# Block norms of attention keys and queries: from one f32 product per segment to two fp32r products of a split square

## The chip, the cores and the metric

The kernel runs on one core of one Trainium2 chip. The metric is device microseconds of one execution, from runs of the whole kernel. The engines are named as the profile names them: PE (TensorE matmul), PEld (its weight load), DVE (VectorE), ACT (ScalarE), POOL (GpSimd) and SP (SyncE, which issues most DMAs).

## The reference

One layer of a hybrid backbone on 1280 tokens (256 context tokens, then 1024 latent tokens on a grid 64 wide) of width 1024. Modulated RMSNorm, one input projection, two head groups side by side, one output projection with a gated residual, then a SwiGLU feed-forward with its own gated residual.

```
q, k, v, z, a, b = ...                         # group A: gated DeltaNet, 4 heads of 128, both directions
o = delta(q, k, v) fwd + bwd                   # chunks, each with a triangular solve
q = rms_norm(q, q_norm_w) * NA_HEAD_DIM ** -0.5     # group B: neighbourhood attention, 8 heads of 64
k = rms_norm(k, k_norm_w)                      # mean of squares over the 64 channels of a head
out = softmax(q k^T + bias) v                  # window keys plus all context keys
```

The change is in the two `rms_norm` lines of group B. `rms_norm` divides by the root of the mean of squares over a head's 64 channels, per token.

## The kernel before, in words

Activations lie with channels on the 128 partitions and tokens along the free dimension. A matmul of two f32 operands is written either directly in f32, or as products of operands rounded to fp32r: the normalized input is held as a high and a low part (`hh`, `hl`, eight tiles each of 128 channels), and a weight as `whi`, `wlo` (`load_w`: ACT rounds at L199, POOL or DVE subtracts at L200). A projection block of 128 output channels then takes, for each of the eight input tiles, three products (`mm_part`, L405) into PSUM banks of the tag `blk`, one bank for each segment of tokens. Segments are 256, 512 and 512 tokens; queries have no context tokens and only the two of 512.

The projection is a list of jobs: DeltaNet key blocks k0 to k3 and a wide half of z, then attention keys nk0, nk1, nk2, half of nv (a wide job of values), nk3, DeltaNet queries q0 to q3, attention queries nq0 to nq3, and values. In the loop over jobs, job n's matmuls are emitted, with pieces of the finish of job n-2 (transposes, stores) and of a background list between them; then its banks are evacuated (L438, or L453 into a tile `cr` for a block that has a short convolution, which follows on DVE at L457 and L461), the norm of job n-1 is emitted, and job n's SiLU and square (`silu`, the square lands in a tile `r` of the tag `cr`).

The norm of an nk or nq block: for each segment, one f32 matmul with a block-diagonal mask of ones (two blocks of 64) sums the squares of each head (L492), ACT takes Ln of the bank (L493), then Exp with scale -0.5 (L497), DVE multiplies (L500), ACT and DVE make an f16 high and low part (L505, L506 for keys; L512, L513 for queries), and SP stores both. The banks for the sums have the tag `m`, two buffers, which the transposes and the DeltaNet work also use.

The background list, from nk0 on: `block_inverses`, which builds per-chunk triangular systems and solves them on DVE in a loop of 30 dependent pairs (L885, L887), transposes the result back on PE (L897), and copies it on ACT (L899), with two more multiplies and transposes on DVE (L905, L908); then `preps`, one for each chunk of 128 tokens: POOL masks four tiles `rg` (L957, after six memsets at L931), ACT fills `fx` (L961), PE forms the log decays (L967, L968), ACT takes Exp (L971), DVE multiplies (L974), PE and ACT apply one block of the inverse (L986, L989), and three rounds of small products follow (L997), each copied to `y` by DVE and ACT (L999, L1000) before the next round. The banks of `preps` have the tag `pr`, two buffers. Preps 0 and 1 may start as soon as the inverses are there; the others are held until all q blocks are done. A second background list computes modulation (L219, L221, L232, L234).

Nothing of this is an order written by hand to the end: a list scheduler orders the instructions of each engine, and a tile takes a free buffer of its tag, so a change of durations or of buffers changes the order of all of them. In the tag `cr` two buffers serve the evacuated block and the square; in the tag `kx` three buffers serve the f16 pair `hl16`, the transposed tiles and others.

Of the kernel before, what the change touches and what calls it, by code (L numbers as in the profile page):

```python
# [30 lines left out]
PLAIN = 2  # L31
SEGS = [(0, 256), (256, 512), (768, 512)]

C_ID, C_LE, C_GE, C_BD2, C_ONE = range(5)


def const_arrays():
    p = np.arange(128)[:, None]
    f = np.arange(128)[None, :]
    same = (p // 32) == (f // 32)  # L40
    m = [p == f, p <= f, p >= f, p > f, p < f, (p > f) & same, (p < f) & same]
    big = np.stack([x.astype(np.float32) for x in m[:3] + [(p // 64) == (f // 64)]], 1)
    f32 = np.arange(32)[None, :]
    q = p % 32
    small = np.stack([x.astype(np.float32) for x in
                      [q <= f32, q >= f32, q < f32, q > f32]], 1)
    out = np.concatenate([big.reshape(128, -1), small.reshape(128, -1)], 1)
    masks = np.stack([x.astype(np.float32) for x in m[3:]], 1)
    return np.ascontiguousarray(out), np.ascontiguousarray(masks)


NCONST = 4 * 128 + 4 * 32
WIN = (256, 0)
CTX = {256: slice(0, 256), 0: slice(384, 640)}
PACE = 0.63
# [33 lines left out]
def hybrid(ctx, tc, a, dbg):  # L89
# [26 lines left out]
    def const(name, shape, dt=F32):  # L116
        return mid.tile(shape, dt, name=name, tag=name)
# [4 lines left out]
    sel = bias[:, 4:6]  # L122
    act.dma_start(sel, a["sel"])
    cst = const("cst", [128, NCONST])
    M = [cst[:, i * 128:(i + 1) * 128] for i in range(4)] + [ones]
    mc = [cst[:, 512 + i * 32:512 + (i + 1) * 32] for i in range(4)]
    ident = M[C_ID]
    n1w, n2w, bada = prm[:, 0:8], prm[:, 8:16], prm[:, 16:64]
    cw = const("cw", [128, 12, 5])
# [4 lines left out]
    for i, v in enumerate((EPS, -0.5 * math.log(64.0))):  # L134
        dve.memset(bias[:, i:i + 1], v)
    b_eps, b_naq = bias[:, 0:1], bias[:, 1:2]
    mr = const("mr", [128, 5, 128], F32R)
    mneg = const("mneg", [128, 2, 128], F32R)

    v_d = dram.tile([T, 512], F32, name="v_d", tag="v_d")  # L140
# [234 lines left out]
    with ExitStack() as bs:  # L375
# [32 lines left out]
        class Block:  # L408
# [56 lines left out]
            def silu(self):  # L465
                acc, t0 = self.acc, self.t0
                if self.kind in "qkv":
                    act.activation(acc[:, t0:], acc[:, t0:], AF.Silu)
                if self.kind in ("q", "nq", "nk"):
                    self.r = cp.tile([128, T], F32, name="cr", tag="cr", bufs=2)  # L470
                    act.activation(self.r[:, t0:], acc[:, t0:], AF.Square)

            def norm(self):

                kind, acc, t0, i = self.kind, self.acc, self.t0, self.i
                if kind == "v":
                    return
                if kind == "k":
                    sp.dma_start(kT_d[:, :, i], acc.rearrange("p (c t) -> p c t", t=128))
                    return  # L480
                r = self.r
                if kind == "q":
                    sp.dma_start(qT_d[:, :, i], acc[:, t0:].rearrange("p (c t) -> p c t", t=128))
                    p = bank()
                    for c in range(8):
                        pe.matmul(p[:, c:c + 1], r[:, t0 + c * 128:t0 + (c + 1) * 128], M[C_ONE][:, 0:1],
                                  start=True, stop=True)
                    dve.tensor_copy(SQ[:, :, i], p[:, 0:8])
                    return
                for s0, n in self.segs:  # L490
                    p = bank()
                    pe.matmul(p[:, :n], M[C_BD2], r[:, s0:s0 + n], start=True, stop=True)  # L492
                    act.activation(r[:, s0:s0 + n], p[:, :n], AF.Ln, bias=b_eps, scale=1.0 / ND)  # L493
                if kind == "nq":
                    act.activation(r[:, t0:], r[:, t0:], AF.Exp, scale=-0.5, bias=b_naq)
                else:
                    act.activation(r[:, t0:], r[:, t0:], AF.Exp, scale=-0.5)  # L497
                isk = kind == "nk"
                u = acc
                dve.scalar_tensor_tensor(u[:, t0:], u[:, t0:], qkw[:, isk:isk + 1], r[:, t0:],  # L500
                                         op0=OP.mult, op1=OP.mult)
                hl16 = cp.tile([128, 2, T], F16, name="hl16", tag="kx", bufs=3)
                h16, l16 = hl16[:, 0], hl16[:, 1]
                if isk:
                    act.copy(h16, u)  # L505
                    dve.tensor_tensor(l16, u, h16, OP.subtract)  # L506
                else:
                    for hf in range(2):
                        s = slice(t0 + hf * 512, t0 + hf * 512 + 512)
                        uv = u[:, s].rearrange("p (r b c) -> p b r c", r=8, b=4)  # L510
                        hv, lv = (x[:, s].rearrange("p (b r c) -> p b r c", b=4, r=8) for x in (h16, l16))
                        act.copy(hv, uv)  # L512
                        dve.tensor_tensor(lv, uv, hv, OP.subtract)  # L513
                for i, x in enumerate((h16, l16)):
                    for hb in range(2):
                        hd = 2 * self.i + hb
                        dst = nk_d[i, hd] if isk else nq_d[hd, i]
                        sp.dma_start(dst, x[hb * 64:hb * 64 + 64, t0:])
# [125 lines left out]
        with ExitStack() as xs:  # L644
            xp = pools(xs, "xp", "left")
            xt = []
            masks = xp.tile([128, 4, 128], F32, name="masks", tag="masks")
            ascope = ExitStack()
            wap = pools(ascope, "wap", "right", 7)
            aw = {}  # L650
# [59 lines left out]
            with tc.manual_schedule(engines={mybir.EngineType.PE, mybir.EngineType.DVE, mybir.EngineType.Activation}):  # L710
                sums = [bank() for _ in SEGS]
                segs = [slice(s0, s0 + n) for s0, n in SEGS]
                for k in range(0, KT, 2):
                    sq = [xp.tile([128, T], F32, name="sq%d" % i, tag="sq%d" % i, bufs=2 + i) for i in range(2)]
                    act.activation(sq[0], xt[k], AF.Square)
                    for s in segs if k == KT - 2 else [slice(0, T)]:
                        act.activation(sq[1][:, s], xt[k + 1][:, s], AF.Square)
                        dve.tensor_tensor(sq[1][:, s], sq[0][:, s], sq[1][:, s], OP.add)
                    for p, s in zip(sums, segs):
                        pe.matmul(p[:, :s.stop - s.start], M[C_ONE], sq[1][:, s], start=k == 0, stop=k == KT - 2)  # L720
                for p, s in zip(sums, segs):
                    act.activation(rs[:, s], p[:, :s.stop - s.start], AF.Ln, bias=b_eps, scale=1.0 / D)
                act.activation(rs, rs, AF.Exp, scale=-0.5)
                first[0].prefetch(raws[0], dve, dve)
                first[1].prefetch(raws[1], pool, pool)
                ada(0, dve.tensor_copy)
                column(0)
                normed_tile(0, segs)
                ada(1, act.copy)
                for b in first:  # L730
                    b.banks()
                for j, (w, x) in enumerate(((0, hh), (1, hh), (0, hl))):
                    for b in first:
                        for o, s in b.outs:
                            pe.matmul(o, b.w[w][:, 0], x[0][:, s], start=j == 0, stop=False)
                        if j == 0 and b is first[1]:
                            column(1)
                            normed_tile(1)
                ada(2, act.copy)
                column(2)  # L740
                for k in range(1, KT):
                    if k == 3:
                        ascope.close()
                        h_tiles(pools(bs, "hp2", "right"), 4)
                    if k + 1 < KT:
                        normed_tile(k + 1)
                    for j, b in enumerate(first):
                        b.mm([k])
                        for q in AHEAD.get((k, j), ()):
                            if q in rows:  # L750
                                column(q)
                            else:
                                ada(q, act.copy)
                    if k == 5:
                        act.copy(mr[:, 4], ident)
                        for d in range(2):
                            act.mul(mneg[:, d], masks[:, d], -1.0e30)
                        act.copy(mr[:, 0:4], masks)

        cp = pools(bs, "cp", "right")  # L760
        late = ExitStack()
# [155 lines left out]
        def preps():  # L917

            first_half.close()
            with ExitStack() as gs:  # L920
# [28 lines left out]
                def prep(i, got):  # L949
# [14 lines left out]
                    for d, c, kk, xc, at in got:  # L964
                        p = bank("pr")
                        for j in range(2):
                            pe.matmul(p, mr[:, d], fl(rgs[2 * d + j]), start=j == 0, stop=False)  # L967
                        pe.matmul(p, mr[:, 4], mneg[:, d].rearrange("p (o i) -> p o i", o=1).to_broadcast(  # L968
                            [128, 4, 128]), start=False, stop=True)
                        e = work("e", 2)  # L970
                        act.activation(fl(e), p, AF.Exp)  # L971
# [803 lines left out]
```

## Time and profile before

| what | value |
|---|---|
| median of three runs | 1557.04 us (1555.83 to 1560.87) |
| profiled execution | 1556.61 us |
| its span, first to last instruction | 1554.8 us |
| mean granted PE clock | 0.979 of full |
| busy: PE, DVE, ACT, POOL | 1486.3, 993.5, 727.8, 234.1 us |
| nk and nq blocks, where the change is | between about 177 and 550 us of the span |

The busy time of PE is 96% of the span, so what is not hidden behind PE shows as a gap in its row of a window, and a lower granted clock shows as longer matmuls. Group rows give the work of an instruction group; waits name who was waited for; a window row gives the busy time of the five engines in a stretch, with the granted clock.

### The profile page before, as it was taken

How to read it: one execution, taken by the hardware profiler on the slowest of the kernel's cores; microseconds unless marked ns; L12 is line 12 of the kernel's file. 1: busy time of each engine (PE TensorE's matmuls, PEld its weight loads, DVE VectorE, ACT ScalarE, POOL GpSimd, SP SyncE). 2: the span in 40 equal slices, each digit the busy share in tenths (PEclk: the TensorE clock that was granted, in tenths of full speed). 3: DMA queues.
4: the chain of work that ended last, by engine and by line, in shares of the span. 5: the costliest groups of instructions: out<-in, count | busy, mean ns of one | idle time of the engine just before them, and what ended most of it. 6: DMA issues, size and time to landing. Idle time of an engine off the chain costs nothing. (4 is left out here: it accounts for less than half of the span.)

```text
span 1554.8 us, 23965 instructions
## 1 busy us (share of the span) xinstructions
PE 1486.3 (96%) x8702; PEld 1239.4 (80%) x8702; DVE 993.5 (64%) x1712; ACT 727.8 (47%) x1404; POOL 234.1 (15%) x286
## 2 busy tenths in 40 slices
PE   6999999999899978999999999999999999999998
PEld 4788787677678858888887878888888888888887
DVE  5774496674454544667986559865666656689652
ACT  5442552535754336665874266333333334454440
POOL 1154500733625110111210000000000000000000
PEclk9999998899989979999999999999999999999999
DMA  9274221578545466888737601632222224698742
GB/s 388 62 222 126 72 75 55 163 228 241 191 145 183 137 186 193 298 275 265 241 101 246 228 34 59 225 107 105 102 102 102 103 101 156 228 376 290 243 143 82
DMA packets 204118, 267.35 MB, mean 172 GB/s; under 512 B 16736, under 2 KB 114528, under 8 KB 202976
## 3 DMA queue, kind: packets, MB, share of 16 engines
q1 hardware_dynamic: 198480, 261.07, 50.7%
q10 hardware_dynamic: 5520, 4.76, 0.9%
q8 instruction: 68, 1.11, 0.3%
q14 instruction: 50, 0.41, 0.1%
HBM read 201.02 MB, written 68.94 MB: 174 GB/s over the span
## 5 line engine op out<-in xcount | busy, mean ns | idle before, releaser
L405 PE MATMUL blk<-hh,whi 128*128 128x512 f32 (+1 forms) x410 | 124.3, 396 | 2.4 <-ACT kk L550 1.4
L1412 ACT CAST uhi<-wq 128x512 fp32r<-128x512 f32 x101 | 61.0, 622 | 131.9 <-issue 84.9
L1412 ACT CAST uhi<-ws 128x512 fp32r<-128x512 f32 x91 | 54.0, 621 | 146.4 <-PE ps L1351 96.5
L405 PE MATMUL blk<-hl,whi 128*128 128x512 f32 (+1 forms) x410 | 117.5, 379 | 0.3 <-DVE hl L707 0.3
L595 PE MATMUL blk<-zw,hh 128*128 128x256 f32 (+1 forms) x576 | 115.2, 294 | 0.9 <-ACT kk L550 0.8
L405 PE MATMUL blk<-hh,wlo 128*128 128x512 f32 (+1 forms) x410 | 115.1, 378 | 0.6 <-POOL wlo L200 0.6
L1413 DVE TENSOR_TENSOR ulo<-wq,uhi 128x512 fp32r<-128x512 f32 x101 | 67.6, 687 | 58.8 <-ACT uhi L1412 32.4
L1351 PE MATMUL ps<-hT,uhi 128*128 128x512 f32 x336 | 103.6, 390 | 0.0
L1351 PE MATMUL ps<-lT,uhi 128*128 128x512 f32 x336 | 103.5, 389 | 0.0
L1351 PE MATMUL ps<-hT,ulo 128*128 128x512 f32 x336 | 103.5, 389 | 0.0
L595 PEld LDWEIGHTS blk<-zw,hh 128*128 128x128 f32 x576 | 93.0, 193 | 4.7 <-issue 2.0
L1351 PE MATMUL ps<-hB,uhi 128*128 128x512 f32 x288 | 89.2, 391 | 0.6 <-ACT hB L1526 0.6
L1351 PE MATMUL ps<-lB,uhi 128*128 128x512 f32 x288 | 88.8, 389 | 0.4 <-DVE lB L1527 0.4
L1351 PE MATMUL ps<-hB,ulo 128*128 128x512 f32 x288 | 88.7, 389 | 0.0
L405 PEld LDWEIGHTS blk<-hh,wlo 128*128 128x128 f32 x410 | 72.7, 193 | 15.4 <-POOL wlo L200 0.9
L405 PEld LDWEIGHTS blk<-hh,whi 128*128 128x128 f32 x410 | 69.9, 194 | 18.6 <-issue 4.5
L405 PEld LDWEIGHTS blk<-hl,whi 128*128 128x128 f32 x410 | 72.9, 193 | 14.5 <-DVE hl L707 0.8
L595 PE MATMUL blk<-zw,hl 128*128 128x256 f32 (+1 forms) x288 | 83.5, 290 | 0.0
L1351 PEld LDWEIGHTS ps<-hT,ulo 128*128 128x128 f32 x336 | 63.1, 188 | 13.2
L1351 PEld LDWEIGHTS ps<-lT,uhi 128*128 128x128 f32 x336 | 63.1, 188 | 13.1
L1351 PEld LDWEIGHTS ps<-hT,uhi 128*128 128x128 f32 x336 | 62.9, 188 | 12.9
L200 POOL TENSOR_TENSOR wlo<-wraw,whi 128x1024 fp32r<-128x1024 f32 x18 | 45.3, 2517 | 180.6 <-ACT whi L199 173.2
(359 smaller groups left out, 3544.5 us busy)
## 6 DMA issues: line engine op xcount, KB each, us to landing
wq<-w_fo SPq DMA_DIRECT2D x99, 256.0 KB, 4.3
wq<-w_gu SPq DMA_DIRECT2D x88, 256.0 KB, 2.8
wad<-wa SPq DMA_DIRECT2D x64, 256.0 KB, 4.6
bt<-rpb SPq DMA_DIRECT2D x64, 192.0 KB, 3.5
t_d<-g SPq DMA_DIRECT2D x22, 512.0 KB, 3.6
fr<-t_d SPq DMA_DIRECT2D x44, 256.0 KB, 5.1
f_d<-g SPq DMA_DIRECT2D x33, 256.0 KB, 2.1
fr<-f_d SPq DMA_DIRECT2D x33, 256.0 KB, 4.1
```

Source lines behind the costliest of these rows:

```text
L200: lo_engine.tensor_tensor(o, r, h.bitcast(F32), OP.subtract)
L405: pe.matmul(o, ww[:, k], xx[k][:, s], start=k == 0 and j == 0, stop=k == KT - 1 and j == 2)
L595: pe.matmul(p[:, :c1 - c0], x[k][:, s], ww[:, k, c0:c1], start=k == 0 and j == 0, stop=k == KT - 1 and j == 2)
L1351: pe.matmul(o, w[wi][:, k], x[xi][:, k], start=first and k == 0 and j == 0, stop=k == n - 1 and j == 2, skip_group_check=True)
L1412: act.copy(hi, self.raw[key])
L1413: dve.tensor_tensor(lo, self.raw[key], hi.bitcast(F32), OP.subtract)
```

## The change

The squares `r` of nk and nq blocks are split: ACT rounds `r` into `rh` (fp32r, a new tile of the tag `cr`, which still has two buffers), and DVE subtracts, which gives `rl` (a new tile of the tag `kx`, which still has three). Each segment's sum is then two fp32r products, of `rh` and of `rl`, accumulated in the bank, instead of one f32 product. The block-diagonal mask moves from the f32 constants `cst` into the fp32r masks `mr` (slot 4; the identity goes to slot 5). The third segment of a key block takes its bank from the tag `pr` instead of `m`.

```diff
             def silu(self):
...
                     act.activation(self.r[:, t0:], acc[:, t0:], AF.Square)
+                if self.kind in ("nq", "nk"):
+                    self.rh = cp.tile([128, T], F32R, name="crh", tag="cr", bufs=2)
+                    self.rl = cp.tile([128, T], F32R, name="crl", tag="kx", bufs=3)
+                    act.copy(self.rh[:, t0:], self.r[:, t0:])
+                    dve.tensor_tensor(self.rl[:, t0:], self.r[:, t0:], self.rh[:, t0:].bitcast(F32), OP.subtract)
...
-                for s0, n in self.segs:
-                    p = bank()
-                    pe.matmul(p[:, :n], M[C_BD2], r[:, s0:s0 + n], start=True, stop=True)
+                for j, (s0, n) in enumerate(self.segs):
+                    p = bank("pr" if j == 2 else "m")
+                    for h, x in enumerate((self.rh, self.rl)):
+                        pe.matmul(p[:, :n], mr[:, 4], x[:, s0:s0 + n], start=h == 0, stop=h == 1)
                     act.activation(r[:, s0:s0 + n], p[:, :n], AF.Ln, bias=b_eps, scale=1.0 / ND)
...
-                        act.copy(mr[:, 4], ident)
+                        act.copy(mr[:, 5], ident)
...
-                        act.copy(mr[:, 0:4], masks)
+                        act.copy(mr[:, 0:5], masks)
...
-                        pe.matmul(p, mr[:, 4], mneg[:, d].rearrange("p (o i) -> p o i", o=1).to_broadcast(
+                        pe.matmul(p, mr[:, 5], mneg[:, d].rearrange("p (o i) -> p o i", o=1).to_broadcast(
```

Line numbers after the edit are 5 higher from `silu` on and 6 higher from the end of the loop over segments: L492 becomes L498, L500 L506, L885 L891, L897 L903, L957 L963, L967 L973, L986 L992, L997 L1003.

The order of instructions differs between about 177 and 550 us of the span before, and is the same again after that. Three places follow. In the names, `hh_`, `hl_` with a number are the input tiles (in the order of the eight k tiles of a block, 129 first and 458 last), `whi`, `wlo` the weight's parts, and `blk`, `m`, `pr` the banks.

PE before, at the end of q1 (`hh_458`, `hl_459`) and the start of q2 (`hh_129`):

```order
L405 MATMUL blk<-hh_458,whi 128x512
L967 MATMUL pr<-rg,mr 128x512
L405 MATMUL blk<-hh_458,whi 128x512
L967 MATMUL pr<-rg,mr 128x512
L968 MATMUL pr<-mneg,mr 128x512
L967 MATMUL pr<-rg,mr 128x512
L405 MATMUL blk<-hl_459,whi 128x512
L967 MATMUL pr<-rg,mr 128x512
L968 MATMUL pr<-mneg,mr 128x512
L405 MATMUL blk<-hl_459,whi 128x512
L405 MATMUL blk<-hh_458,wlo 128x512 x2
L405 MATMUL blk<-hh_129,whi 128x512 x2
```

The products of preps 0 and 1 stand between those of q1, and the rest of these two preps stands in the same way between those of q2 and q3.

PE in the changed kernel, at the end of q1:

```order
L405 MATMUL blk<-hl_459,whi 128x512 x2
L405 MATMUL blk<-hh_458,wlo 128x512 x2
L973 MATMUL pr<-rg,mr 128x512 x2
L974 MATMUL pr<-mneg,mr 128x512
L973 MATMUL pr<-rg,mr 128x512 x2
L974 MATMUL pr<-mneg,mr 128x512
L992 MATMUL pr<-fx_2248,kk 128x128 x4
L992 MATMUL pr<-fx_2249,kk 128x128 x4
L1003 MATMUL pr<-y_2250,kk 32x32 x4
L1003 MATMUL pr<-y_2251,kk 32x32 x4
```

and, 20 rows on, at the start of q2:

```order
L1003 MATMUL pr<-y_2252,kk 32x96
L1003 MATMUL pr<-y_2253,kk 32x96
L498 MATMUL pr<-crh,mr 128x512
L498 MATMUL pr<-crl,mr 128x512
L973 MATMUL pr<-rg,mr 128x512 x2
L974 MATMUL pr<-mneg,mr 128x512
L405 MATMUL blk<-hh_129,whi 128x512
L405 MATMUL blk<-hl_130,whi 128x512
```

Between the last product of q1 and the first of q2 there is now all of preps 0 and 1, then the third segment of nk3 (the one whose bank is `pr`), then the first products of prep 2.

ACT before, around the copy of q0's banks (`cr<-blk`):

```order
L899 COPY WK<-m 128x80x4 x8
L199 CAST whi<-wraw 128x1024
L453 COPY cr<-blk 128x512 x2
L493 ACT_TABLE_LOAD
L493 ACTIVATE cr<-m,bias 128x256
L493 ACTIVATE cr<-m,bias 128x512 x2
L497 ACT_TABLE_LOAD
```

and in the changed kernel:

```order
L995 COPY kk<-pr 128x512 x2
L1006 COPY y_2253<-pr 32x4x32
L1006 COPY y_2253<-pr 32x4x64
L967 COPY fx_2248<-xc 32x4x32
L1006 COPY y_2253<-pr 32x4x96
L967 COPY fx_2248<-xc 32x4x32 x2
L453 COPY cr<-blk 128x512 x2
L499 ACT_TABLE_LOAD
L499 ACTIVATE cr<-pr,bias 128x512
```

The copy of q0's banks stood right behind the copies of the inverses (L899). It now stands behind those of prep 1 (L1006), beside the Ln of nk3's third segment. A `blk` bank that it reads is written next by q2.

In words, since only a count differs there: on POOL, the run of subtractions L200 ahead of the six memsets has five in place of four (the fifth is of q3's weight, whose cast on ACT waits for a buffer that q1's matmuls read); on DVE, the subtractions of nk2 and nk3 that make `rl` stand between the pairs of the inverse's loop, those of nk0 and nk1 ahead of it.

More of the change, by code (lines that the diff above doesn't have):

```diff
@@ L32 @@
 SEGS = [(0, 256), (256, 512), (768, 512)]
-C_ID, C_LE, C_GE, C_BD2, C_ONE = range(5)
+C_ID, C_LE, C_GE, C_ONE = range(4)
 def const_arrays():
@@ L41, in const_arrays @@
     m = [p == f, p <= f, p >= f, p > f, p < f, (p > f) & same, (p < f) & same]
-    big = np.stack([x.astype(np.float32) for x in m[:3] + [(p // 64) == (f // 64)]], 1)
+    big = np.stack([x.astype(np.float32) for x in m[:3]], 1)
     f32 = np.arange(32)[None, :]
@@ L47, in const_arrays @@
     out = np.concatenate([big.reshape(128, -1), small.reshape(128, -1)], 1)
-    masks = np.stack([x.astype(np.float32) for x in m[3:]], 1)
+    masks = np.stack([x.astype(np.float32) for x in m[3:] + [(p // 64) == (f // 64)]], 1)
     return np.ascontiguousarray(out), np.ascontiguousarray(masks)
-NCONST = 4 * 128 + 4 * 32
+NCONST = 3 * 128 + 4 * 32
 WIN = (256, 0)
@@ L124, in hybrid @@
     cst = const("cst", [128, NCONST])
-    M = [cst[:, i * 128:(i + 1) * 128] for i in range(4)] + [ones]
-    mc = [cst[:, 512 + i * 32:512 + (i + 1) * 32] for i in range(4)]
+    M = [cst[:, i * 128:(i + 1) * 128] for i in range(3)] + [ones]
+    mc = [cst[:, 384 + i * 32:384 + (i + 1) * 32] for i in range(4)]
     ident = M[C_ID]
@@ L136, in hybrid @@
     b_eps, b_naq = bias[:, 0:1], bias[:, 1:2]
-    mr = const("mr", [128, 5, 128], F32R)
+    mr = const("mr", [128, 6, 128], F32R)
     mneg = const("mneg", [128, 2, 128], F32R)
@@ L646, in hybrid @@
             xt = []
-            masks = xp.tile([128, 4, 128], F32, name="masks", tag="masks")
+            masks = xp.tile([128, 5, 128], F32, name="masks", tag="masks")
             ascope = ExitStack()
```

## The prediction

> **What bounds the kernel now.** The profiled execution took 1556.61 us, 0.4 below the median of 1557.04; times below are positions in its span, and a shift found there is added to the median. I read the page's busy times first, then PE's waits and the windows of the stretch in which the order changes. The page:
>
> ```profile
> PE 1486.3 (96%) x8702; PEld 1239.4 (80%) x8702; DVE 993.5 (64%) x1712; ACT 727.8 (47%) x1404; POOL 234.1 (15%) x286
> ```
>
> So 69 us of the span are PE gaps. Whom PE waited for between 150 and 460 us (total, times, longest):
>
> ```profile
> PE m L492 <- ACT cr L493: 5.3, 4, 1.4
> PE pr L997 <- DVE y L999: 4.8, 3, 2.7
> PE pr L997 <- ACT kk L989: 3.5, 2, 2.9
> PE m L897 <- DVE N L891: 2.9, 1, 2.9
> PE pr L967 <- POOL rg L957: 2.5, 2, 1.3
> ```
>
> The first row is what the other bank removes: a key block's third segment waits until Ln has read the first one's bank. The fourth is PE waiting for the inverses. The others belong to preps. Windows (PE, PEld, DVE, ACT, POOL busy; then granted clock):
>
> ```profile
> 194.66:257.09 62.43, 56.91 (x370) 50.05 (x368) 59.80 (x63) 23.91 (x34) 5.45 (x2) 1.00 0.20 60
> 260.00:283.00 23.00, 21.73 (x94) 17.31 (x93) 13.44 (x8) 10.15 (x15) 5.15 (x7) 0.82 0.29 109
> 283.00:321.00 38.00, 33.60 (x222) 25.74 (x221) 25.33 (x25) 20.34 (x40) 27.21 (x29) 0.87 0.56 176
> 321.00:371.43 50.43, 48.96 (x271) 41.97 (x270) 32.40 (x50) 20.87 (x33) 11.71 (x11) 1.00 0.82 249
> 371.43:460.00 88.57, 77.63 (x519) 60.14 (x519) 44.18 (x49) 62.08 (x108) 46.86 (x54) 0.98 0.59 184
> 460.00:540.00 80.00, 79.69 (x601) 68.95 (x598) 36.12 (x48) 31.18 (x70) 25.51 (x37) 0.96 0.54 167
> ```
>
> From 195 to 257 us DVE, with the inverse's loop, is the full engine (59.80 of 62.43). Preps 0 and 1 run from 283 to 321 under q1 and q2, and PE idles only 4.4 us there. In 371 to 460, under nq0 to nq3, PE idles 10.9 us. After 460 PE is full, and after 550 the order is the same in both kernels: a shift that stands then stays.
>
> **1. The products.** PE around nq0's norm, start and duration:
>
> ```profile
> 370.97 0.62 PE L405 MATMUL blk<-hh,wlo 128*128 128x512 f32 x2
> 371.43 1.88 PE L492 MATMUL m<-cr,cst 128*128 128x512 f32 x4
> 372.75 1.03 PE L405 MATMUL blk<-hh,whi 128*128 128x512 f32 x2
> 373.62 0.62 PE L405 MATMUL blk<-hl,whi 128*128 128x512 f32 x2
> ```
>
> Two fp32r products of 512 columns take 0.46 (370.97 to 371.43). The two f32 sums are four records; from 371.43 to 373.62 are 2.19 us, less 0.46 for the pair behind them: 1.73. Four fp32r products cost 0.92, so an nq block saves 0.81, an nk block, with 1280 columns for 1024, 1.01. Eight blocks: 7.3 us. With the 5.3 of the first wait, 12.6 us, if PE sets the pace everywhere. It doesn't.
>
> **2. The inverses come later.** ACT and DVE get one instruction more per block; the nearest rows are the square (ACT) and the f16 subtraction (DVE):
>
> ```profile
> L471 ACT ACTIVATE cr<-cacc 128x1280 f32<-128x1280 f32 x4 | 5.1, 1278 | 0.0
> ```
> ```profile
> L506 DVE TENSOR_TENSOR hl<-cacc,hl 128x1280 f16<-128x1280 f32 x4 | 6.8, 1695 | 1.3 <-ACT hl L505 1.3
> ```
>
> Keys: 1.28 on ACT and 1.5 to 1.7 on DVE; queries four fifths. nk0's and nk1's subtractions fall ahead of the loop, into DVE's idle time; those of nk2 and nk3 stand in it, where DVE is full: +3.0. nk1's cast stands on ACT between copies that feed the loop: +1.0. Against that, the work ahead of the loop comes up to 0.5 sooner.
>
> ```profile
> 257.09 0.45 PE L897 MATMUL m<-cst,N 80*128 80x80 f32 x2 [2.89 <-DVE N L891]
> ```
>
> These products move from 257.1 to 260.6 (258 to 263: without the cast's 1.0 and half a subtraction, or with two subtractions held up). PE, which saves 3.0 on three key blocks and 4.0 of their stalls, comes sooner and waits longer: what the keys gain is lost here.
>
> A subtraction beside POOL could cost more:
>
> ```profile
> 200.18 2.84 DVE L885 TENSOR_TENSOR tt<-N 80x600 f32<-80x600 f32 x1
> ```
> ```profile
> 248.86 0.78 DVE L885 TENSOR_TENSOR tt<-N 80x600 f32<-80x600 f32 x1
> ```
>
> The same shape took 2.84 where POOL ran an L200, 0.78 alone. The Trainium skill, "SBUF — State Buffer", section "Who interferes with whom", says that a DVE instruction with two SBUF inputs contends with a POOL instruction that reads SBUF; these two rows agree, and by it each new subtraction beside an L200 would cost some 2 us more. I count no such meeting, and put it in the upper end.
>
> **3. Preps 0 and 1 stand alone.** Before, from the inverses (257.09) to q2's first product it took 35.4 us:
>
> ```profile
> 291.60 1.05 PE L405 MATMUL blk<-hh,wlo 128*128 128x512 f32 x2
> 292.45 1.05 PE L405 MATMUL blk<-hh,whi 128*128 128x512 f32 x2
> ```
>
> In the new order 21 of q0's products are done ahead of the inverses (21 x 0.23 = 4.8), nk3's sum is two segments at the new price (saves 1.5), six prep products (1.4) and waits of 1.3 (L492) and 2.5 (`rg`) go, and q1 ends ahead of the slow-clock stretch at 288 (1.9). That is 22.0: q1 ends near 282.6. Then comes the term that decides. Before, ACT and POOL did this when q0 ended:
>
> ```profile
> 270.47 1.04 ACT L199 CAST whi<-wraw 128x1024 fp32r<-128x1024 f32 x1 [6.04 <-PE blk L405]
> 271.42 1.07 ACT L453 COPY cr<-blk 128x512 f32<-128x512 f32 x2
> ```
> ```profile
> 271.59 2.37 POOL L200 TENSOR_TENSOR wlo<-wraw,whi 128x1024 fp32r<-128x1024 f32 x1 [18.87 <-ACT whi L199]
> 273.90 0.99 POOL L931 MEMSET fx<- 128x512 f32 x2
> 274.83 1.92 POOL L931 MEMSET y<- 128x512 f32 x4
> 283.10 1.59 POOL L957 TENSOR_TENSOR rg<-GH,cst 128x512 fp32r<-128x512 f32 x1 [6.36 <-DVE WK L908]
> ```
>
> The cast waits until a block's products free the buffer. POOL's fifth L200 now waits in the same way for q3's cast, thus for q1's end, with the memsets and `rg` queued behind it: 282.6 + 1.05 + 2.37 + 2.9 = 288.9 for the first `rg`, where q1 has no product left to cover it. The rest of the chain has these prices:
>
> ```profile
> L957 POOL TENSOR_TENSOR rg<-GL,cst 128x512 fp32r<-128x512 f32 x6 | 9.1, 1513 | 0.0
> L957 POOL TENSOR_TENSOR rg<-GH,cst 128x512 fp32r<-128x512 f32 x6 | 8.2, 1367 | 10.8 <-DVE WK L908 6.4 <-PE pr L967 4.4
> ```
> ```profile
> L971 ACT ACTIVATE e<-pr 128x512 f32<-128x512 f32 x4 | 2.4, 604 | 0.2 <-PE pr L968 0.2
> L989 ACT COPY kk<-pr 128x512 f32<-128x512 f32 x4 | 2.3, 585 | 2.9 <-PE pr L986 2.8
> ```
> ```profile
> L974 DVE TENSOR_TENSOR kk<-kk,e 128x512 f32<-128x512 f32 x4 | 3.7, 936 | 4.6 <-ACT e L971 4.6
> ```
> ```profile
> L999 DVE COPY y<-pr x6: 289/417/546, 299.7 to 320.7; 32x128 f32<-32x128 f32 x2, 32x256 f32<-32x256 f32 x2, 32x384 f32<-32x384 f32 x2
> ```
> ```profile
> 311.06 1.97 PE L986 MATMUL pr<-fx,kk 128*128 128x128 f32 x16
> 312.95 0.44 PE L997 MATMUL pr<-y,kk 128*32 128x32 f32 x8
> ```
>
> Prep 0: four `rg` 5.8, products 0.7, Exp 0.60, multiply 0.94, four products 0.5 (16 in 1.89), copy 0.59, then three rounds of products at about 0.4 and copies of 0.29, 0.42, 0.55: 11.6. Prep 1's products and copies from the inverse on: 0.95 + 1.17 + 2.4 = 4.5. Then nk3's third segment 0.46, and the first copy of q0's bank (L453), now behind all that on ACT, 0.54, before q2 may write the bank: 17.1. Some 22 handovers at 0.1 (the last of the 16 products ends at 313.03, its copy starts at 313.1) add 2, and half clock on the 6 us of products some 4.4, since PE mostly waits. In all 23.5 (18 to 30): q2 starts at 312.4 in place of 292.45.
>
> The clock row for that half price, around the earlier wait (clock third from the right):
>
> ```profile
> 256.00:260.00 4.00, 2.91 (x16) 2.52 (x17) 1.71 (x6) 0.85 (x2) 0.00 (x0) 0.74 0.00 0
> 260.00:268.00 8.00, 8.00 (x35) 6.85 (x34) 3.00 (x2) 2.55 (x6) 0.00 (x0) 0.50 0.21 84
> 268.00:272.00 4.00, 4.00 (x17) 2.89 (x17) 0.00 (x0) 1.53 (x3) 0.41 (x1) 0.98 0.41 164
> ```
>
> After a wait of 2.9 us the clock was 0.50 for 8 us of full work. The Trainium skill, "TensorE: Matmul & The Clock Gate", section "Part 1: The HAM clock gate", has half rate after an idle window of about 3.4 us, and full rate again after about 3.4 us of sustained work; the first half the trace bears out, the second only roughly (8 us at 0.50 here). By its shorter ramp the sum would be some 2 us less than by the row.
>
> **4. What comes back.** From q2's start to nq0's norm were 79.0 us. From it go the preps' products that are now done (9.4: 32 of L986 at 0.12, 96 of L997 about 4.2, six `rg` products 1.4) and the wait for `y` of about 1.9; prep 2's first products come in (1.2). That leaves 68.9: nq0's norm moves from 371.4 to 381.3, +9.9. Behind it: prep 2's front is done (-1.9), its waits in L986 go (-1.5, an estimate from the preps' waits above), the four nq savings of 0.81 are worth 2.0 of 3.2, since PE waited 10.9 of these 88.6 us for chains that a faster sum doesn't shorten (0 to 3.2), and four casts and subtractions on engines in these chains cost 2 (0 to 6). Together +6.5: **1563.5 us**. By the bounds of q2's start (-5, +6.5) and of these two terms (-3, +6), this case holds 1555 to 1576.
>
> **The rivals.** A, faster: PE sets the pace, and the whole 12.6 us arrive: 1544.4. It speaks for it that the stalls and the f32 price are in the rows. It speaks against it that DVE gates PE at 257 and that the new order has no q product beside preps 0 and 1. The result is even if q2 starts at 305.9 (312.4 less 6.5), faster by over 0.3% (4.7 us, about what a measurement of this kernel can tell) if before 301; for the full gain at 293.
>
> B, about the same: q1 ends at 279 and the chain takes 20, with a full clock; q2 starts at 305.3 and the result is 1556.4.
>
> C, slower still: half clock through the chain and past q2's start (8 us at half, +4), subtractions beside POOL in the loop (+2), and chains of nq that wait for casts (+4): 1573.5. The price of the first is the row at 260; what speaks against the last is that ACT was busy only 62 of 88.6 us.
>
> D: fp32r products of the mask run at f32's pace, and nothing is saved on PE: 1563.5 + 2.0 + 1.0 (nk3) = 1566.5. The rows of L405 speak against it.
>
> **How the numbers follow.** Forecast 0.50, A 0.17, B 0.15, C 0.16, D 0.02. Faster takes A; same B and 0.07 of the forecast's lower end; slower the remaining 0.43 of it, C and D: 0.61. The range leaves out A and the top of C: 1551 to 1575, where the lower end takes in a q2 start at 300.
>
> **What would show it.** Right: PE idle or waiting for L963, L980, L995 or L1005 for about 20 us between q1's last L405 and q2's first, clock near 0.5 there; L903's first products near 260; four records of L498 in 0.9 us; no wait for L499 in key blocks; nq0's norm near 381. Wrong: q2's first L405 before 301, or a shift that is still undone between 460 and 550.

## The result, and the profile after

The changed kernel takes 1567.22 us (1566.15 to 1569.63) against 1557.36 us before (1555.83 to 1560.87): the ratio is 1.0064, with a 95% interval of 1.0046 to 1.0081. It is slower by 9.9 us, where 6.5 were forecast. The profiled execution took 1567.25 us, its span is 1565.5, its mean granted clock 0.975 (before 0.979).

Busy times of the page. PE has 3.6 us less work and the span is 10.7 us longer, so the gaps grew by 14:

```profile
PE 1482.7 (95%) x8702; PEld 1244.3 (79%) x8702; DVE 1004.6 (64%) x1720; ACT 737.9 (47%) x1414; POOL 235.6 (15%) x286
```

Whom PE waited for between 150 and 480 us, the longest rows. The rows of Ln (now L499) are gone. First is the wait for `rg`, with 7.3 us in one piece, second the wait for the inverses, 5.4 where it was 2.9. The third is new: the q norms wait for their squares.

```profile
PE pr L973 <- POOL rg L963: 8.2, 3, 7.3
PE m L903 <- DVE N L897: 5.4, 1, 5.4
PE m L491 <- ACT cr L471: 4.6, 2, 2.8
PE pr L1003 <- ACT kk L995: 4.2, 1, 4.2
PE pr L992 <- DVE y L1005: 3.5, 2, 2.4
```

The same windows as before (PE, PEld, DVE, ACT, POOL busy; granted clock third from the right). PE's idle time rose in the windows from 260 to 371 us: 2.7 in the second (before 1.3), 10.2 in the third (before 4.4), 4.6 in the fourth (before 1.5); in the last two of these the clock fell, from 0.87 to 0.82 and from 1.00 to 0.86. In the first window, ahead of the inverses, PE idled less than before (1.5 in place of 5.5); that window ends before the wait for them is over.

```profile
194.66:257.09 62.43, 60.93 (x402) 55.24 (x400) 58.83 (x57) 27.33 (x38) 5.14 (x2) 1.00 0.21 60
260.00:283.00 23.00, 20.26 (x98) 16.75 (x98) 10.03 (x15) 7.64 (x13) 3.39 (x2) 0.85 0.40 138
283.00:321.00 38.00, 27.80 (x183) 21.54 (x184) 17.18 (x19) 22.88 (x48) 33.01 (x53) 0.82 0.69 215
321.00:371.43 50.43, 45.81 (x233) 40.13 (x232) 31.25 (x37) 21.02 (x30) 7.98 (x4) 0.86 0.60 180
371.43:460.00 88.57, 80.02 (x513) 64.85 (x512) 51.04 (x59) 60.01 (x102) 41.65 (x43) 0.96 0.59 186
```

PE from the inverses to q2 and on to the norm of nq0. The inverses' first products start at 260.98; q1's last pair starts at 280.62; the first product of prep 0 waits 7.29 us; behind prep 1 comes nk3's third segment at 311.07, then q2 at 312.39; nq0's sum begins at 387.24:

```profile
260.98 0.53 PE L903 MATMUL m<-cst,N 80*128 80x80 f32 x2 [5.39 <-DVE N L897]
...
280.62 0.61 PE L405 MATMUL blk<-hh,wlo 128*128 128x512 f32 x2
288.53 0.79 PE L973 MATMUL pr<-rg,mr 128*128 128x512 f32 x1 [7.29 <-POOL rg L963]
...
311.07 0.50 PE L498 MATMUL pr<-crh,mr 128*128 128x512 f32 x1 [0.49 <-DVE y L1005]
...
312.39 0.50 PE L405 MATMUL blk<-hh,whi 128*128 128x512 f32 x1
...
387.24 0.50 PE L498 MATMUL m<-crh,mr 128*128 128x512 f32 x1
```

Why `rg` came so late is seen on POOL. The fifth L200 starts after the cast of q3's weight, which waited for q1's last products, and six memsets and `rg` follow without a gap:

```profile
281.99 2.70 POOL L200 TENSOR_TENSOR wlo<-wraw,whi 128x1024 fp32r<-128x1024 f32 x1 [13.29 <-DMA x_d<-ut]
284.63 0.99 POOL L937 MEMSET fx<- 128x512 f32 x2
285.56 1.91 POOL L937 MEMSET y<- 128x512 f32 x4
287.45 1.03 POOL L963 TENSOR_TENSOR rg<-GH,cst 128x512 fp32r<-128x512 f32 x1
```

The row's own releaser is a DMA that had long been done; the cast is in ACT's timeline:

```profile
280.87 1.05 ACT L199 CAST whi<-wraw 128x1024 fp32r<-128x1024 f32 x1 [8.55 <-PE blk L405]
```

And q0's copy, with the rows around it, stands behind the last copy of prep 1:

```profile
310.61 0.47 ACT L1006 COPY y<-pr 32x384 f32<-32x384 f32 x1 [0.68 <-PE pr L1003]
311.11 0.62 ACT L967 COPY fx<-xc 32x128 f32<-32x128 f32 x2
311.75 1.07 ACT L453 COPY cr<-blk 128x512 f32<-128x512 f32 x2
```

It was at 271.42 before. Between 550 us and the end the shift stays as it is: the feed-forward's first products start at 912.3 before and 923.4 after, its last group at 1351.8 and 1362.9, 11.1 us in both places; the spans differ by 10.7.

### The profile page after: what moved, and what is told of

It reads as the page before. It is cut to its first block, busy times and chain, and to the rows that moved or that the text cites. A ratio compares the mean times of both kernels' runs of the same rounds, so it can differ in the third digit from the quotient of the medians.

```text
span 1565.5 us, 23997 instructions
## 1 busy us (share of the span) xinstructions
PE 1482.7 (95%) x8702; PEld 1244.3 (79%) x8702; DVE 1004.6 (64%) x1720; ACT 737.9 (47%) x1414; POOL 235.6 (15%) x286
## 5 line engine op out<-in xcount | busy, mean ns | idle before, releaser
L405 PE MATMUL blk<-hh,whi 128*128 128x512 f32 (+1 forms) x410 | 120.7, 389 | 1.4 <-ACT kk L556 1.4
L405 PE MATMUL blk<-hl,whi 128*128 128x512 f32 (+1 forms) x410 | 116.6, 378 | 0.3 <-DVE hl L713 0.3
L405 PE MATMUL blk<-hh,wlo 128*128 128x512 f32 (+1 forms) x410 | 114.6, 375 | 0.6 <-POOL wlo L200 0.6
L405 PEld LDWEIGHTS blk<-hl,whi 128*128 128x128 f32 x410 | 73.3, 194 | 14.4 <-DVE hl L713 0.8
L405 PEld LDWEIGHTS blk<-hh,wlo 128*128 128x128 f32 x410 | 72.6, 193 | 14.7 <-POOL wlo L200 0.9
L405 PEld LDWEIGHTS blk<-hh,whi 128*128 128x128 f32 x410 | 70.3, 194 | 15.9 <-issue 1.6
L200 POOL TENSOR_TENSOR wlo<-wraw,whi 128x1024 fp32r<-128x1024 f32 x18 | 44.9, 2494 | 221.8 <-ACT whi L199 173.1
```

The costliest lines, as they stand in the source:

```text
L200: lo_engine.tensor_tensor(o, r, h.bitcast(F32), OP.subtract)
L405: pe.matmul(o, ww[:, k], xx[k][:, s], start=k == 0 and j == 0, stop=k == KT - 1 and j == 2)
```

## The experiments

The prediction had named the place of the loss, not which edit makes the scheduler put it there. Two edits could: the rounded square takes the second buffer of `cr` (the split), and nk3's third sum takes its bank from `pr`, whose two banks the preps hold in turn. All ratios below are to the kernel before, run on the same chip (medians of 1557.7, 1558.1 and 1558.4 us in the three sets), with their 95% intervals. They are the ratios on record and not the quotients of the medians: these agree within 0.0005 in the last two sets, but lie 0.0008 to 0.0019 higher in the first (experiments 1 to 4). A difference of two ratios carries the uncertainty of both, some 0.25% to 0.45% either way, or 4 to 7 us (an estimate from the intervals). Positions in two profiles are not to be compared to the microsecond either: nk0's first sum stands at 177.7 us before and 178.0 in the changed kernel, but at 182.0 in the first experiment and 175.5 in the fourth.

**1. nk3's third bank back in `m`.**

```diff
-                    p = bank("pr" if j == 2 else "m")
+                    p = bank("pr" if j == 2 and i < 3 else "m")
```

> The changed kernel with one difference: the third segment of the last key block nk3 takes its bank from m again (those of nk0, nk1, nk2 stay in pr). Then nk3's norm no longer stands behind preps 0 and 1 on PE, its rounded square frees its buffer of cr before the preps, and q0's copy and q2's products go ahead of the preps. Theory (the loss is preps 0 and 1 standing alone, because that copy waits for nk3's rounded square): the inverses' products stay near 261, no gap of 20 us follows q1, and about 11 us come back and more: 1552 to 1557. Rival 1 (the casts and subtractions, which this kernel keeps whole, make the loss by loading ACT and DVE): 1563 to 1567.

1552.48 us, 0.9948 (0.9923 to 0.9972). One bank of one block turns a loss of 0.6% into a gain of 0.5% (0.3% by the medians). The split itself is whole in this kernel, so the load of casts and subtractions is not the loss. In its timeline q0's banks are copied 38 us sooner than in the changed kernel (first row; the other two are q1's):

```profile
273.68 1.07 ACT L453 COPY cr<-blk 128x512 f32<-128x512 f32 x2
288.39 0.57 ACT L453 COPY cr<-blk 128x512 f32<-128x512 f32 x1
297.80 0.58 ACT L453 COPY cr<-blk 128x512 f32<-128x512 f32 x1
```

**2. The rounded square in `kx`, nk3's bank in `pr`.**

```diff
-                    self.rh = cp.tile([128, T], F32R, name="crh", tag="cr", bufs=2)
+                    self.rh = cp.tile([128, T], F32R, name="crh", tag="kx", bufs=3)
```

> The changed kernel with one difference: the rounded square is a tile of the tag kx in place of cr; nk3's third segment stays in pr and still stands behind preps 0 and 1 on PE. Theory (it is the buffer of cr that holds q0's copy back, not the bank): the preps lie among q2's products again, 1552 to 1557. Rival 1 (load of ACT and DVE): 1563 to 1567. Rival 2 (the bank: nk3's sum in pr, by itself, holds the rest): also 1563 to 1567, with PE waiting around nk3's sum.

1561.58 us, 1.0016 (0.9997 to 1.0036). This is a miss: the buffer of `cr` is only part of it, some 40% of the way from the change (1.0064) to the first experiment (0.9948). The gap ahead of q2 is gone, and q0's and q1's banks are copied by 286 us. But nk3's sum is still at 310.59, behind the preps, and its norm holds another thing that q1 needs. DVE's timeline shows which: q1's convolution (L457) writes into a tile `cacc`, of which there are two, and starts right behind the last instruction of nk3's norm that reads one of them (L512):

```profile
314.98 1.55 DVE L506 SCALAR_TENSOR_TENSOR cacc<-cacc,qkw,cr 128x1280 f32<-128x1280 f32 x1 [4.70 <-ACT cr L503]
319.06 1.61 DVE L512 TENSOR_TENSOR hl<-cacc,hl 128x1280 f16<-128x1280 f32 x1 [2.53 <-ACT hl L511]
320.70 0.75 DVE L457 TENSOR_SCALAR cacc<-cr,cw 128x1024 f32<-128x1024 f32 x1
```

So a late norm of nk3 holds back q0 through `cr` (in the change) or, as the code and these three rows have it, q1 through `cacc` (here). The delay moves by one block. That `cacc` makes the rest is argued from this and not shown: no run gave it a third buffer.

**3. The bank alone**, in the kernel before: one f32 product, third segments of all key blocks in `pr`.

```diff
-                for s0, n in self.segs:
-                    p = bank()
+                for j, (s0, n) in enumerate(self.segs):
+                    p = bank("pr" if j == 2 else "m")
                     pe.matmul(p[:, :n], M[C_BD2], r[:, s0:s0 + n], start=True, stop=True)
```

> The kernel before with the bank alone: one f32 product per segment from the square itself, no split, third segment of key blocks in pr. Theory: cr holds only the square, so q0's copy goes ahead; the stalls of the third segments go (5.3 us), but what lies ahead of the inverses is lost waiting for them there: 1553 to 1558. Rival 2 (the bank alone makes the loss): 1563 to 1568.

1559.97 us, 0.9996 (0.9978 to 1.0014): no difference that can be told; by the ratio it is at the upper edge of what the theory gave, by the median 2 us above. The stalls are gone, and the wait for the inverses is 5.7 in place of 2.9. The same delay as in the second experiment stands here: nk3's sum at 316.41, q1's convolution at 326.45 (308.26 before). So the bank costs nothing that can be told without the split: it is the two together that lose.

**4. No low part.** The subtraction and the second product are left out.

```diff
-                    dve.tensor_tensor(self.rl[:, t0:], self.r[:, t0:], self.rh[:, t0:].bitcast(F32), OP.subtract)
...
-                    for h, x in enumerate((self.rh, self.rl)):
-                        pe.matmul(p[:, :n], mr[:, 4], x[:, s0:s0 + n], start=h == 0, stop=h == 1)
+                    pe.matmul(p[:, :n], mr[:, 4], self.rh[:, s0:s0 + n], start=True, stop=True)
```

> The changed kernel without the low part (left out: the subtraction and its product; the sums are those of the rounded squares alone). cr and pr are as in the change, and preps 0 and 1 stand alone behind q1 as there. Theory: the inverses come 3 us sooner, eight subtractions and 20 products are saved, and the gap stays: 1559 to 1565. Rival 1 (the subtractions on DVE make the loss): 1550 to 1556.

1556.94 us, 0.9987 (0.9966 to 1.0008): by the median between the two expectations, by the ratio (some 1555 us) inside the rival's. The inverses come at 257.08, 3.9 us sooner than in the changed kernel; 2.6 of this is the loop, which takes 61.9 us from its start to the inverses in place of 64.5, and the loop also starts 1.3 sooner. The gap stays: PE waits 7.1 us for `rg` in one piece, and nk3's sum is at 307.90. By the ratios the low part costs 0.77% in the changed kernel, some 12 us, against 3.9 of the inverses and 4.1 of its products (9216 columns at 0.23 us for 512). The remaining 4 us are within the width of the two intervals, so whether there is a rest at all stays open.

**5. All banks in `m`**, so the split alone: `p = bank("m")` in the loop.

> The changed kernel with the split alone: every segment's bank from m, as before. Theory (the loss comes from nk3's third sum in pr, which stands behind preps 0 and 1 and holds buffers of cr until then; the other three key blocks' banks matter little, since what PE saves ahead of the inverses it waits for there): within 2 us of the version with only nk3 in m, a ratio of 0.993 to 0.998, 1549 to 1555. Rival (the three stalls of nk0 to nk2, 4 us, count): 0.998 to 1.001.

1550.72 us, 0.9952 (0.9933 to 0.9971): as in the first experiment, though the stalls of nk0 to nk2 are back. What PE loses in them it waits less for the inverses, 3.2 us in place of 5.4 in the first experiment. The two rows of waits in this kernel:

```profile
PE m L498 <- ACT cr L499: 5.2, 4, 1.4
PE m L903 <- DVE N L897: 3.2, 1, 3.2
```

**6. The split for queries alone**, all banks in `m`, keys with the f32 product.

```diff
-                if self.kind in ("nq", "nk"):
+                if self.kind == "nq":
...
+                    if kind == "nq":
                         for h, x in enumerate((self.rh, self.rl)):
                             pe.matmul(p[:, :n], mr[:, 4], x[:, s0:s0 + n], start=h == 0, stop=h == 1)
+                    else:
+                        pe.matmul(p[:, :n], mr[:, 4].bitcast(F32), r[:, s0:s0 + n], start=True, stop=True)
```

> The split for the attention queries alone; keys as before, with one f32 product from the square and all banks from m. The inverses are not delayed (257), nothing is added to DVE there. Theory (queries' products of 3.2 us are saved, part is given back to casts and to chains that are not shorter): 0.997 to 0.9995, 1553 to 1557. Rival (casts and subtractions of the queries cost more than they save): 1.000 to 1.003.

1549.93 us, 0.9948 (0.9931 to 0.9964). The queries alone give all that the whole split gives, and some 8 us where I had expected 1 to 5, so both expectations missed; the excess over 3.2 us of products is not fully explained (see the last section).

**7. The first version without the low part** (left out as in the fourth).

> The version with only nk3's third bank in m, and without the low part (left out: eight subtractions and 20 products; the sums are those of the rounded squares). It prices the low part where no chain stands alone. Theory: 3 us from the inverses and 4.2 us of products, of which about half shows: 0.990 to 0.994, 1543 to 1549. Rival (the low part is free beside other work): 0.994 to 0.997, as with it.

1543.34 us, 0.9905 (0.9869 to 0.9941): by the ratios the low part costs 0.43%, 6.7 us, beside the first experiment. That it is not free beside other work is likely and not shown, since the two intervals overlap and this version has four runs. Against the fourth experiment, whose only difference is nk3's bank, it is 0.82%, 13 us; the same bank costs 1.16%, 18 us, between the change and the first experiment (14 and 15 us by the medians).

**8. The keys' subtractions on POOL** (the first version, with `pool` for `dve` there).

> The version with only nk3's third bank in m, with the keys' subtractions on POOL in place of DVE. DVE has 3.0 us less in the inverse's loop, POOL runs 3 us more per block there, and a DVE pair beside it takes up to 2 us longer. Theory: the two about cancel, the inverses come at 258 to 262 in place of 261 to 263.5, 0.992 to 0.996. Rival (POOL beside the loop costs DVE more than 3 us): inverses after 263, 0.996 to 1.000.

1560.55 us, 1.0020 (1.0002 to 1.0037): slower than even the rival had it. The inverses come at 270.31 and PE waits 9.1 us for them. Not all of the 6.8 us beyond the first experiment (263.50) is the loop. 1.8 stand already at the first product of the wide half of z (112.4 against 110.6), ahead of any subtraction. 2.4 come before the loop starts: nk0's subtraction stands at 172.08 in POOL's queue ahead of the last `rc` tiles of `block_inverses` (L849), and PE waits 2.54 us for these in place of 0.93. The loop itself takes 67.2 us to the inverses, against 64.5 with the subtractions on DVE in it and 61.9 without any (experiment 7): so POOL beside it costs DVE some 5 us, more than the 3.0 it saves. A subtraction takes 3.28 us on POOL:

```profile
L476 POOL TENSOR_TENSOR crl<-cr,crh 128x1280 fp32r<-128x1280 f32 x4 | 13.1, 3281 | 10.5 <-ACT crh L475 10.5
```

Two instructions of the loop that met one (it ran from 220.32 and from 258.63) took 3.76 and 3.54 us, in place of 1.03 and 0.92 alone. Here the rule of the Trainium skill, "SBUF — State Buffer", section "Who interferes with whom", which the prediction drew on, is borne out: a DVE instruction with two inputs from SBUF is held while POOL reads there.

```profile
221.01 3.76 DVE L891 TENSOR_TENSOR tt<-N 80x840 f32<-80x840 f32 x1
...
258.83 3.54 DVE L893 TENSOR_TENSOR N<-N,tt 80x736 f32<-80x736 f32 x1
```

**9. Only nk3's bank in `pr`**, the reverse of the first: `bank("pr" if j == 2 and i == 3 else "m")`.

> The split, with the third bank of nk3 alone in pr and those of nk0, nk1, nk2 in m: the reverse of the first experiment. Theory (nk3's sum in pr stands behind preps 0 and 1, and its square and rounded square hold both buffers of cr until then): the whole loss is back, q2 starts near 312, ratio 1.004 to 1.009. Rival (the other three banks, or the four together, make it): 0.994 to 1.000.

1565.40 us, 1.0041 (1.0024 to 1.0058). The loss is back with this bank alone: 0.89%, 14 us, against the fifth experiment. In its profile, which is the fastest of its ten runs (1559.13), prep 0 waits 7.46 us for `rg` at 288.04, nk3's sum is at 309.48 and q2 at 310.80:

```profile
288.04 0.79 PE L973 MATMUL pr<-rg,mr 128*128 128x512 f32 x1 [7.46 <-POOL rg L963]
...
309.48 0.50 PE L498 MATMUL pr<-crh,mr 128*128 128x512 f32 x1 [0.49 <-DVE y L1005]
...
310.80 0.49 PE L405 MATMUL blk<-hh,whi 128*128 128x512 f32 x1
```

**10. The split for keys alone**, nk3's bank in `m`, those of nk0 to nk2 in `pr`.

> The split for the keys alone, with nk3's third bank in m and those of nk0 to nk2 in pr; queries have one f32 product as before. Theory (what the keys save is waited off at the inverses, which their two subtractions delay by 3 to 4 us): 0.998 to 1.002. Rival (the keys' products, 4.0 us, and the stalls of 4 us count): 0.994 to 0.997.

1553.94 us, 0.9973 (0.9962 to 0.9985), between the expectations: alone the keys give some 4 us, a part of their 4.0 of products and the 4.0 of stalls. PE waits 5.4 us for the inverses. Beside the queries' split they add nothing (experiments 1 and 5 against 6).

**11. The split for queries, with the banks of nk0 to nk2 in `pr`.**

> The split for the queries alone, with one f32 product for the keys, and the third banks of nk0 to nk2 in pr (nk3's in m). Theory: the three stalls go, but PE waits as much longer for the inverses: as with the queries alone, 0.993 to 0.997. Rival (the stalls count): 0.990 to 0.993.

1550.63 us, 0.9952 (0.9934 to 0.9970), as the theory had it: the stalls are gone, and PE waits 5.7 us for the inverses in place of 2.9.

With the sums whole, experiments 1, 5, 6, 10 and 11 thus beat the kernel before. Those with the queries split reach 1550 to 1552 us, whether the keys are split too (1 and 5) or not (6 and 11); the keys' split lengthens the chain of the inverses and adds nothing to that.

## Why the prediction was right, step by step

- **Products (step 1).** Right. The four fp32r products of nq2 start 0.23 us apart, 0.92 in all, against 1.73. PE's busy time fell by 3.6 us in place of 7.3; matmuls at a slower clock count as more of it (a pair of L405 takes 0.61 us at full clock and 1.05 at 0.50), and the mean clock fell from 0.979 to 0.975. PE at nq2's sum:

```profile
425.89 0.39 PE L498 MATMUL m<-crh,mr 128*128 128x512 f32 x1
426.12 0.40 PE L498 MATMUL m<-crl,mr 128*128 128x512 f32 x1
426.35 0.39 PE L498 MATMUL m<-crh,mr 128*128 128x512 f32 x1
426.58 0.39 PE L498 MATMUL m<-crl,mr 128*128 128x512 f32 x1
426.81 0.74 PE L405 MATMUL blk<-hh,whi 128*128 128x256 f32 x3
```

- **The inverses (step 2).** Forecast 260.6, measured 260.98. The keys' subtractions took 1.48 us, a cast 1.26; PE came early and waited, as said. The sum held better than its terms: the loop starts 1.8 us later (0.5 forecast) and grows by 2.1 (3.0 forecast). And one subtraction did meet POOL, nk0's ahead of the loop: it took 2.33 us. Experiments 3, 5 and 11 show the same exchange of stalls for waiting.
- **Preps standing alone (step 3).** q1 ended at 281.2 (282.6), `rg` began at 287.45 (288.9), from there to q2 were 24.9 us (23.5), q2 began at 312.39 (312.4). The mechanism is the one forecast, but the hit to a tenth is luck: q1 ended 1.4 us sooner and the chain took 1.4 longer. Nor did PE idle for about 20 us in it, as the signs had it: between q1's last product and q2's first it idled 12.0 of 31.2 us, 7.3 of them in the wait for `rg`, and from prep 0's first product on (288.53) 4.7 of 23.9. The clock was 0.50 only at the chain's start and full from 304 us; its mean from 288.53 to q2 was 0.80, which makes at most 4.8 us of loss (an estimate: 0.20 of 23.9), near the 4.4 of the term for half clock:

```profile
288.00:292.00 4.00, 2.61 (x5) 1.10 (x5) 1.16 (x2) 1.00 (x2) 4.00 (x5) 0.50 0.96 306
292.00:296.00 4.00, 3.53 (x16) 3.03 (x17) 2.02 (x2) 2.62 (x7) 3.79 (x6) 0.67 0.91 280
296.00:300.00 4.00, 2.47 (x35) 2.24 (x34) 0.41 (x2) 2.95 (x10) 3.73 (x9) 0.76 0.02 7
300.00:304.00 4.00, 4.00 (x27) 2.96 (x25) 2.50 (x4) 1.56 (x3) 3.60 (x8) 0.81 0.42 122
```

- **What comes back (step 4).** The term that was mis-sized. nq0's norm was forecast at 381.3 and came at 387.2, a shift of 15.8 in place of 9.9. Missing in the sum was that the late copy of q0's banks (311.75) delays its convolution on DVE and so its square: PE waited 2.8 us for it (L491 at 327.98) and 1.84 for q2's at 359.82, where DVE has the work of the modulation between the steps of the convolution. Behind both waits the clock was slow again: 0.60 and 0.55 from 328 to 336, and 0.50 from 364 to 368. Of the shift of 15.8, 5.6 came back by nq3's norm (446.12 before, 456.35 after: 10.2), more than the 3.4 that I had counted. So the error at nq0 was 5.9 and at the end 3.4, and the nearness of the final number owes something to two errors of opposite sign. The two waits:

```profile
327.98 2.85 PE L491 MATMUL m<-ones,cr 128*128 128x1 f32 x16 [2.78 <-ACT cr L471]
...
359.82 1.95 PE L491 MATMUL m<-ones,cr 128*128 128x1 f32 x16 [1.84 <-ACT cr L471]
```

- **The rivals.** A fell because DVE gated PE at 261 and because no q product lay beside the preps; with nk3's bank in `m`, experiments 1, 5 and 6 reach 7 to 8 of its 12.6 us by the ratios (5 to 8 by the medians). B's chain of 20 us took 24.9, and not at full clock. C had the right sign for the clock, but the chains of nq did not lose: from nq0's sum to nq3's it took 69.1 us, 74.7 before. D fell with the 0.23 us from one product of nq2 to the next. On the clock, the prediction took its row at 260 us as bearing out half rate after an idle window of about 3.4 us; the wait ahead of that row was 2.89 us, so the row shows a slow clock behind a wait, and not that length (see the last section).
- **What the prediction left open:** which edit makes the order. It is one bank of one block, together with the split (experiments 1, 3, 5 and 9). nk3's norm, with a bank of `pr`, is queued behind preps 0 and 1, and until it is done it holds `r`, the rounded square and `cacc`, for which the q blocks wait.

## What to carry to other kernels

A bank or buffer taken from a pool that a long chain uses is not free because it is free at that moment: whoever takes it is queued behind that chain, and what it holds elsewhere is held as long. So ask of each moved tile which other tiles its owner keeps until it is served, and who needs those next. And an instruction that PE saves counts only where PE is late last: ahead of a wait for another engine it is waited off.

## What the runs showed of the hardware

A wait of the same length can, or need not, bring the slow clock. In the kernel before, 2.89 us of waiting for the inverses were followed by some 10 us at 0.50 (258 to 268); in the sixth experiment's profile, with a wait of 2.94 us at the same place, the clock stayed full:

```profile
254.00:258.00 4.00, 3.42 (x15) 2.46 (x14) 3.90 (x4) 1.46 (x2) 2.00 (x1) 1.00 0.07 20
258.00:262.00 4.00, 1.64 (x12) 1.50 (x12) 2.92 (x8) 0.23 (x1) 0.00 (x0) 1.00 0.37 111
262.00:266.00 4.00, 4.00 (x31) 3.63 (x31) 0.00 (x0) 2.96 (x8) 0.00 (x0) 1.00 0.00 0
```

That alone is some 5 us of a run (an estimate: 10 us at half), and the runs of one kernel differ by more: 28 of the kernel before lay between 1551.76 us (mean clock 0.989) and 1563.92 (0.979). The sixth experiment's excess over its products does not come from this place alone: the eleventh has the slow clock there in its profile (0.50 from 258 to 266) and is as fast. Another place differs in both. From nk3's last sum to nq0's first, where the queries' split has no product, it took 97.1 us before, 94.0 in the sixth and 94.4 in the eleventh; PE idled 5.9, 5.8 and 6.1 us of it, and the granted clock was 0.95, 0.98 and 0.98. So some 3 us of the excess are slow clock in that stretch, in one profile of each; whether the new order brings this or chance is not shown. The Trainium skill, "TensorE: Matmul & The Clock Gate", section "Part 1: The HAM clock gate", has a window of activity that runs freely, and half rate after at least one idle window of about 3.4 us. Neither wait is as long as that, so the slow clock behind the first does not follow from the page's figure. A window that is not tied to the wait would let the same wait fall into one window or across two, with two outcomes as in these two profiles; no run here tests it.
